# Seven products of a Winograd group in another order on TensorE, its copies and one weight split a step later

## The chip, the cores and the metric

The kernel runs on one core of a Trainium2 chip. The metric is the time of one execution in device microseconds (us). A core has four computing engines that work through queues of their own and wait for each other by semaphores: TensorE (PE in the profile: matmuls into PSUM; its weight loads are shown apart as PEld), VectorE (DVE), ScalarE (ACT) and GpSimd (POOL). SyncE (SP) issues DMAs. PE, DVE, ACT and SP execute their instructions in the order in which the kernel records them.

## The reference

One layer of an encoder over 320 rows (256 of a new stream, 64 of a running one, which share all weights), D_MODEL = 2048, D_FF = 5632:

```python
proj = rmsnorm(x, norm_mix) @ w_in                 # q k v, u v_s, g_a g_b
a  = stick_breaking(q, k, v)                       # 8 heads x 128
bb = spatial_gate(gelu(u), rmsnorm(gelu(vs)))
merged = sigmoid(g_a) * (a @ w_branch_a) + sigmoid(g_b) * (bb @ w_branch_b)
h  = x + merged @ w_out
gu = rmsnorm(h, norm_ffn) @ w_gate_up
h  = h + (silu(gu[..., :D_FF]) * gu[..., D_FF:]) @ w_down
return rmsnorm(h, norm_final), k, v, vs
```

All is float32. The change lies in the last product pair, `w_gate_up` and `w_down`.

## The kernel before

Features lie on partitions and the T = 320 rows on the free axis. A weight block is 128 output columns by K rows. Float32 weights arrive by DMA as a raw tile of 128 x 2048 (`raw`) and are split into two float16 halves that add up to the scaled weight: ScalarE makes the high half (`high`, L381) and VectorE the low half (`low`, L384), both into one tile `w`, of which there are three (`SPLIT`). A power-of-two scale comes first: ScalarE sums absolute values (`bound`, L211, written to `junk`), VectorE packs the result (`pack`, L217 and L219, tile `packed`), TensorE spreads it over partitions (`spread`, L223, tile `row`), VectorE turns it into `up` and `down` (`close`, L227 to L229). Activations are split into float16 halves in the same way. An ordinary block (`Group.block`) then takes three products per 128 rows of K, at L109 to L111.

Some pairs of blocks go through a class of their own, `Fast`: a Winograd form of a 2 x 2 block product. A group takes two blocks (gate and up of one column block, or two blocks of `w_down`) with 16 (or 12) pieces of K, and uses sums of weight pieces (`sum_up`, L425, VectorE, four sums, tile `sum`) and of activations (`mix`, tile `mix`). There are 40 groups: a run of 8 with gate and up; a run of 18, of which the first 6 are of `w_down` (a down group) and 12 of gate and up (an up group); a run of 4 down and 8 up groups; and two down groups with K = 12 x 128 that stand alone between ordinary blocks, near the end. Of a group TensorE makes nine pieces, which get short names here:

- chain products, all accumulated in one half of the PSUM tile `acc` ("first" in the code): A1 (weight as it is), A2 (with sum 2), A3 (with sum 3)
- the other product B (with sum 1), in the other half of the same PSUM tile
- G, the high halves of the gate block in whole (L429), G1 and G2, products into the first and second half of the gate's PSUM tile (an `aux`); U and U1, the same for the up block's tile (another `aux`)

A1, A2, A3, B, G1, G2 and U1 are 16 matmuls of 160 columns each (L435, `cross`); G and U are 16 matmuls of 320 columns (L429, `whole`). ScalarE reads the chain between its products: copy K0 after A1 and copy K1 after A2 (`keep_state`, L440, tile `seen`), copy K2 after A3, negated, into the up block's tile (L442), and copy KB of B's half (`take_other`, L478, tile `bb`). K2 comes before U, which accumulates on it. VectorE joins the copies to the products afterwards (`join`, L482 to L485); then up groups take Silu on ScalarE (L1212) and a product on VectorE (L1220), and down groups add both results to the residual on VectorE (L1228, twice).

The order of each queue is made by a step counter. `tick()` advances it and records the actions that were put at that step with `at(step, action, rank)`, in the order of their ranks; an action that is called outright stands where the code reaches it. A Fast group takes four steps, with a `tick()` at the end of each. `at(s - 3, self.high, ...)` thus puts a high half three steps before its group's start. A group's loads are recorded 11 and 10 steps ahead of its start, its two `bound` 9 and 7, its `pack`, `spread` and `close` 7, 5 and 4 steps ahead.

Of the kernel before, what the change touches and what calls it, by code (L numbers as in the profile page):

```python
# [13 lines left out]
AF = mybir.ActivationFunctionType  # L14
ALU = mybir.AluOpType

P = 128
TP = 256
TS = 64
T = TP + TS  # L20
# [32 lines left out]
def stream_step(ctx: ExitStack, tc: tile.TileContext, xT, w_in, w_a, w_b, w_out, w_gu, w_down,  # L53
                gains, ws_t, bs, ck_t, cv, y_t, k_t, v_t, sv_t):
    nc = tc.nc
# [8 lines left out]
    def acc():  # L64
        return psum.tile([P, 512], F32, tag="acc", bufs=3, name="acc")

    def aux():
        return psum.tile([P, 512], F32, tag="aux", bufs=4, name="aux")
# [8 lines left out]
    def at(tick, fn, *a, rank=5):  # L77
        if tick <= state["tick"]:
            fn(*a)
        else:  # L80
            later.setdefault(tick, []).append((rank, fn, a))

    def tick():
        state["tick"] += 1
        for _, fn, a in sorted(later.pop(state["tick"], ()), key=lambda x: x[0]):
            fn(*a)

    def after(n, fn, *a, rank=5):
        if n == 0:
            fn(*a)  # L90
        else:
            at(state["tick"] + n, fn, *a, rank=rank)
# [20 lines left out]
    class Plain:  # L113

        def __init__(self, src, nk, start):
            self.src, self.nk, self.start, self.w = src, nk, start, {}
            for j, k0 in enumerate(range(0, nk, HALF)):
                at(start + j - 8, self.load, j, rank=0)
                at(start + j - 2, self.high, j, rank=1)
                at(start + j - 1, self.low, j, rank=1)  # L120
# [25 lines left out]
    def slot(shape=(T,), dt=F32R, name="S"):  # L146
        return big.tile([P, *shape], dt, tag="S", bufs=SLOTS, name=name)
# [28 lines left out]
    def t320(tag, bufs=2, dt=F32):  # L176
        return tmp.tile([P, T], dt, tag=tag, bufs=bufs, name=tag)
# [219 lines left out]
    class Fast(Group):  # L397
# [3 lines left out]
        def __init__(self, units, n, start, undo, late_undo=False):  # L401
            self.units, self.undo_of, self.w, self.raw, self.sums, self.start = units, undo, {}, {}, {}, start
            self.n, self.half = n, n // 2
            self.width = [n * P] * 2
            for u, src in enumerate(units):
                s = start + u
                at(s - 11, self.load, u, src, 0, n, rank=0)
                at(s - 9 + u, self.bound, u, False, rank=0.9 if u else 4)
                at(s - 3, self.high, u, rank=2)
                at(s - 2, self.low, u, rank=2)  # L410
            at(start - 7, lambda: self.scale.pack(), rank=3)
            at(start - 5, lambda: self.scale.spread(), rank=1)
            at(start - 4, self.close, late_undo, rank=0.5)
            if late_undo:
                at(start, self.settle, rank=1)
            part = lambda u, j: self.w[u][2][:, :, j * self.half * P : (j + 1) * self.half * P]
            at(start, lambda: self.sum_up(1, part(1, 0), part(1, 1)), rank=2)
            at(start, lambda: self.sum_up(2, part(0, 0), self.sums[1]), rank=3)
            at(start + 1, lambda: self.sum_up(3, part(0, 0), part(1, 0)), rank=0.6)
            at(start + 1, lambda: self.sum_up(4, part(0, 1), self.sums[2]), rank=0.7)  # L420
# [3 lines left out]
            self.sums[i] = t[:, :, : self.half * P]  # L424
            nc.vector.tensor_tensor(out=self.sums[i], in0=a, in1=b, op=ALU.add)  # L425

        def whole(self, ps, u, x, r=None, start=True):
            for k in range(self.n) if r is None else r:
                nc.tensor.matmul(ps[:, :T], self.w[u][0][:, k * P : (k + 1) * P], x.half[k][0], start=start and k == 0,  # L429
                                 stop=False, skip_group_check=True)  # L430

        def cross(self, out, w, j, x, t, start=False, stop=True):
# [12 lines left out]
        def blocks(self, x):  # L445
            assert state["tick"] == self.start
            first, gate, self.up = acc(), aux(), aux()
            part = lambda ps, n: ps[:, n * N : (n + 1) * N]
            if self.n < KD:
                self.seen = slot((2, N), F32, "seen")  # L450
            else:
                turn_of["seen"] = turn_of.get("seen", 0) + 1
                self.seen = tmp.tile([P, 2, N], F32, tag="seen" if turn_of["seen"] % 2 else "sq", bufs=1, name="seen")
            self.chain, self.other = part(first, 0), part(first, 1)
            w0, w1, s, n = self.w[0][2], self.w[1][2], self.sums, self.half
            at(self.start + 2, self.take_other, rank=0.7)
            at(self.start + 2, self.keep_state, 2, rank=0.8)
            self.cross(self.chain, w0, 0, x, 11, start=True)
            self.keep_state(0)
            self.whole(gate, 0, x)  # L460
            self.cross(part(gate, 0), w0, n, x, 21)
            tick()
            self.cross(self.chain, s[2], 0, x, 2)
            self.keep_state(1)
            self.cross(self.other, s[1], 0, x, 1)
            self.cross(self.chain, s[3], 0, x, 3)
            tick()
            self.cross(part(gate, 1), s[4], 0, x, 22)
            self.whole(self.up, 1, x, range(n), False)
            tick()  # L470
            self.whole(self.up, 1, x, range(n, 2 * n), False)
            self.cross(part(self.up, 0), w1, n, x, 4)
            tick()
            return gate[:, :T], self.up[:, :T]
# [461 lines left out]
    start = base + 2 * WHOLE  # L936
    for i, (kind, n) in enumerate(line):
        by_vector = (0,) if 4 <= i < 33 and i % 5 in (1, 3) or i > 40 and i % 3 == 2 else ()
        if kind == "in":
            g = Group([[(w_in[n][:, j * HALF * P : (j + 1) * HALF * P], HALF) for j in range(2)]], start, lambda: [mixed.undo], 11, by_vector)  # L940
        else:
            g = Group([[(w_a[n], H), (w_b[n], H)]], start, lambda: [aT.undo, bT.undo], 11, by_vector, True)
# [3 lines left out]
    whole = Acts(KD)  # L946
# [5 lines left out]
    def block16(n, x):  # L952
        g = groups.pop(("in", n))
        return g.block(0, x), g.undo
# [15 lines left out]
    for i, (name, b, h) in enumerate(heads):  # L970
# [14 lines left out]
        else:  # L985
            ps, undo = block16(b * H + h, mixed.half)
# [16 lines left out]
    for g in range(H):  # L1003
        ps, undo = block16(4 * H + g, mixed.half)
# [67 lines left out]
    for g in range(H):  # L1072
        ps, undo = block16(3 * H + g, mixed.half)
        at(state["tick"] + 1, lambda g=g, ps=ps, undo=undo: nc.scalar.activation(
            out=us[g], in_=ps, func=AF.Gelu_apprx_tanh, scale=undo), rank=2)
# [24 lines left out]
    for m in range(KD):  # L1100
        g = groups.pop(("ab", m))
# [3 lines left out]
        for i, x in enumerate((aT, bT)):  # L1105
            ps = g.block(0, x.half, i * H, H)
# [18 lines left out]
    for made, (kind, s, i) in enumerate(order):  # L1125
        s0, n = SLICES[s]
# [11 lines left out]
        else:  # L1138
            if i % 2 == 0:
                undo = lambda s=s: [acts[s].undo]  # L1140
                if i in FAST_DOWN[s]:
                    g = Fast([w_down[j][:, s0 * P : (s0 + n) * P] for j in (i, i + 1)], n, now, undo, True)
                else:
                    g = Group([pieces(w_down[i], s0, n), pieces(w_down[i + 1], s0, n)], now, undo, 11, (), True, True)
# [21 lines left out]
    for m in range(KD):  # L1166
        x = t320("ev")
        nc.sync.dma_start(out=x, in_=xT[:, m, :])
        ps = outs[m].block(merged) if m < WHOLE_OUT else outs[m].block(0, whole.half)
# [34 lines left out]
    def gated(s, pg, pu, g):  # L1204
        fast = isinstance(g, Fast)
        t, u = g.join(pg, pu) if fast else (t320("ev"), t320("bb"))
        if g is None:
            nc.vector.tensor_tensor(out=t, in0=pg, in1=got["rh"], op=ALU.mult)
            nc.scalar.activation(out=t, in_=t, func=AF.Silu)
            nc.vector.tensor_tensor(out=u, in0=pu, in1=got["rh"], op=ALU.mult)  # L1210
        elif fast:
            after(1, lambda: nc.scalar.activation(out=t, in_=t, func=AF.Silu, scale=g.undo), rank=0.5)  # L1212
        else:
            nc.scalar.activation(out=t, in_=pg, func=AF.Silu, scale=g.undo)
            nc.scalar.activation(out=u, in_=pu, func=AF.Copy, scale=g.undo)

        def out():
            r = slot(dt=F32, name="act")
            if fast:
                nc.vector.scalar_tensor_tensor(out=r, in0=u, scalar=g.undo, in1=t, op0=ALU.mult, op1=ALU.mult)  # L1220
            else:
                nc.vector.tensor_tensor(out=r, in0=u, in1=t, op=ALU.mult)
            acts[s].add(r)

        after(1, out, rank=3)

    def downed(s, i, ps, g):
        nc.vector.scalar_tensor_tensor(out=hs[i], in0=ps, scalar=g.undo, in1=hs[i], op0=ALU.mult, op1=ALU.add)  # L1228
# [26 lines left out]
    for kind, s, i in order:  # L1255
        if kind == "up":
            if i < PLAIN:
                gate_w, up_w = groups.pop((kind, s, i))
                pg, pu, g = gate_w.block(hg), up_w.block(hg), None
            else:  # L1260
                g = groups.pop((kind, s, i))
                pg, pu = g.blocks(ffn) if isinstance(g, Fast) else (g.block(0, ffn.half), g.block(1, ffn.half, bank=aux))
            at(state["tick"] + 1, gated, s, pg, pu, g, rank=2)
            continue
        end = s == 2 and i == KD - 1
        g, u = groups.pop((kind, s, i))
        if isinstance(g, Fast):
            if u == 0:
                ps = g.blocks(acts[s])
                at(state["tick"] + 1, downed_pair, s, i, *ps, g, rank=2)  # L1270
            continue
        if not end:
            ps = g.block(u, acts[s].half)
# [20 lines left out]
        if end:  # L1294
            ps = g.block(u, acts[s].half, into=into)
# [123 lines left out]
```

## Time and profile before

| | us |
|---|---|
| three runs: lowest, median, highest | 1603.80, 1605.57, 1608.05 |
| the profiled execution | 1603.87 |
| its span (2.07 lies around it) | 1601.8 |
| PE busy in the span | 1563.3 (98%) |
| DVE busy | 1262.5 (79%) |
| ACT busy | 1145.7 (72%) |
| POOL busy | 118.2 (7%) |

The mean granted TensorE clock is 0.996. Busy time of PE counts from a matmul's start to its modelled end, and matmuls overlap: a 160-column matmul is shown with 233 ns and is followed 69 ns later by the next. A row of the timeline gives the start, the length, the engine, the line with its operation, the tiles (out<-in), the count of merged instructions, and in brackets the idle time before the first of them with what ended it.

### The profile page before, as it was taken

How to read it: one execution, taken by the hardware profiler on the slowest of the kernel's cores; microseconds unless marked ns; L12 is line 12 of the kernel's file. 1: busy time of each engine (PE TensorE's matmuls, PEld its weight loads, DVE VectorE, ACT ScalarE, POOL GpSimd, SP SyncE). 2: the span in 40 equal slices, each digit the busy share in tenths (PEclk: the TensorE clock that was granted, in tenths of full speed). 3: DMA queues.
4: the chain of work that ended last, by engine and by line, in shares of the span. 5: the costliest groups of instructions: out<-in, count | busy, mean ns of one | idle time of the engine just before them, and what ended most of it. 6: DMA issues, size and time to landing. Idle time of an engine off the chain costs nothing.

```text
span 1601.8 us, 32604 instructions
## 1 busy us (share of the span) xinstructions
PE 1563.3 (98%) x13603; PEld 1262.4 (79%) x13603; DVE 1262.5 (79%) x2149; ACT 1145.7 (72%) x1435; POOL 118.2 (7%) x144
## 2 busy tenths in 40 slices
PE   9999999999999999999999999999999999999997
PEld 9987777777777768879778877888888778887775
DVE  6789887977777766966869858899997688987785
ACT  6589888867666644846767778677776876777773
POOL 0110111100000000221000000000100000000000
PEclk9999999999999999999999999999999999999998
DMA  8567765644444444654544444445444544445341
GB/s 305 202 196 220 197 174 147 193 162 158 159 160 162 162 144 149 204 170 158 203 156 165 159 161 167 147 159 182 165 175 144 173 163 159 159 158 165 122 136 67
DMA packets 89012, 268.63 MB, mean 168 GB/s; under 512 B 27712, under 2 KB 34112, under 8 KB 79136
## 3 DMA queue, kind: packets, MB, share of 16 engines
q1 hardware_dynamic: 86416, 261.36, 49.2%
q0 software_dynamic: 1312, 3.80, 0.7%
q8 instruction: 106, 1.74, 0.4%
q10 hardware_dynamic: 1136, 1.39, 0.2%
q14 instruction: 42, 0.34, 0.1%
HBM read 256.03 MB, written 5.51 MB: 163 GB/s over the span
## 4 chain that ended last, share of the span: by engine, by line
PE 86%; ACT 7%; DVE 4%; issue 2%; DMA 1%; DVEq 0%; POOL 0%; ACTq 0%
PE acc L109 16%; PE acc L111 16%; PE acc L110 16%; PE acc L435 11%; PE aux L429 10%; PE aux L435 7%; ACT w L381 2%; PE aux L109 2%; PE aux L110 2%; PE aux L111 2%; PE aux L573 2%; DVE w L384 1%; ACT junk L211 1%; PE acc L573 1%; ACT seen L440 1%
## 5 line engine op out<-in xcount | busy, mean ns | idle before, releaser
L384 DVE SCALAR_TENSOR_TENSOR w<-raw,up,w 128x2048 f16<-128x2048 f32 (+1 forms) x216 | 498.6, 2308 | 116.7 <-ACT w L381 115.9
L111 PE MATMUL acc<-half,w 128*128 128x320 f16 x1920 | 574.1, 299 | 1.2 <-DVE w L384 1.1
L109 PE MATMUL acc<-half,w 128*128 128x320 f16 x1920 | 574.2, 299 | 0.4 <-DVE gate L1088 0.3
L110 PE MATMUL acc<-half,w 128*128 128x320 f16 x1920 | 574.1, 299 | 0.0
L381 ACT ACTIVATE w<-raw,up 128x2048 f16<-128x2048 f32 (+1 forms) x216 | 424.1, 1964 | 185.8 <-PE acc L111 144.8
L211 ACT ACTIVATE junk<-raw 128x2048 uint8<-128x2048 f32 (+1 forms) x190 | 354.8, 1867 | 5.3 <-DMA raw<-w_out 2.4
L111 PEld LDWEIGHTS <-w 128*128 128x128 f16 x2128 | 208.2, 98 | 82.6 <-DVE w L384 1.8
L109 PEld LDWEIGHTS <-w 128*128 128x128 f16 x2128 | 208.2, 98 | 82.0 <-issue 1.5
L110 PEld LDWEIGHTS <-w 128*128 128x128 f16 x2128 | 208.2, 98 | 77.2 <-issue 0.9
L435 PEld LDWEIGHTS <-sum 128*128 128x128 f16 x2528 | 178.7, 98 | 27.7 <-issue 27.7
L429 PE MATMUL aux<-half,w 128*128 128x320 f16 x1264 | 186.6, 299 | 0.0
L435 PE MATMUL acc<-mix,sum 128*128 128x160 f16 x1896 | 145.5, 234 | 22.3 <-ACT seen L440 22.3
L429 PEld LDWEIGHTS <-w 128*128 128x128 f16 x1264 | 120.0, 98 | 40.7
L435 PEld LDWEIGHTS <-w 128*128 128x128 f16 x1896 | 136.0, 98 | 6.4
L227 DVE TENSOR_REDUCE peak<-row 128x1 f32<-128x128 f32 x156 | 44.5, 285 | 93.1 <-PE row L223 92.9
L425 DVE TENSOR_TENSOR sum<-w,sum 128x2048 f16<-128x2048 f16 (+1 forms) x80 | 96.6, 1207 | 1.6
L425 DVE TENSOR_TENSOR sum<-w 128x2048 f16<-128x2048 f16 (+1 forms) x80 | 96.3, 1204 | 0.3
L372 POOL TENSOR_TENSOR undo<-down,undo 128x1 f32<-128x1 f32 x40 | 37.4, 936 | 527.3 <-DVE down L228 515.7
L131 ACT CAST w<-raw 128x1024 fp32r<-128x1024 f32 x36 | 37.6, 1046 | 44.8 <-PE acc L111 29.5
L109 PE MATMUL aux<-half,w 128*128 128x320 f16 x208 | 62.2, 299 | 0.0
L110 PE MATMUL aux<-half,w 128*128 128x320 f16 x208 | 62.2, 299 | 0.0
L111 PE MATMUL aux<-half,w 128*128 128x320 f16 x208 | 62.2, 299 | 0.0
(268 smaller groups left out, 1954.6 us busy)
## 6 DMA issues: line engine op xcount, KB each, us to landing
raw<-w_in SPq DMA_DIRECT2D x141, 512.0 KB, 4.7
raw<-w_gu SPq DMA_DIRECT2D x56, 1024.0 KB, 4.8
raw<-w_gu SPq DMA_DIRECT2D x64, 512.0 KB, 4.6
raw<-w_down SPq DMA_DIRECT2D x20, 1024.0 KB, 4.9
raw<-w_down SPq DMA_DIRECT2D x36, 512.0 KB, 3.9
raw<-w_out SPq DMA_DIRECT2D x32, 512.0 KB, 4.9
raw<-w_a SPq DMA_DIRECT2D x16, 512.0 KB, 3.8
raw<-w_b SPq DMA_DIRECT2D x16, 512.0 KB, 4.6
```

Source lines behind the costliest of these rows:

```text
L109: nc.tensor.matmul(ps[:, :T], a, x[0], start=first, stop=False, skip_group_check=True)
L110: nc.tensor.matmul(ps[:, :T], a, x[1], start=False, stop=False, skip_group_check=True)
L111: nc.tensor.matmul(ps[:, :T], b, x[0], start=False, stop=last, skip_group_check=True)
L131: nc.scalar.copy(out=self.w[j][0], in_=self.raw[:, j * HALF * P : (j + 1) * HALF * P])
L211: nc.scalar.activation(out=junk, in_=src, func=AF.Abs, accum_out=self.tops[:, i : i + 1])
L227: nc.vector.tensor_reduce(out=top, in_=self.row[:, :P], axis=mybir.AxisListType.X, op=ALU.max)
L381: nc.scalar.activation(out=w[:, 0], in_=self.raw[u][:, : self.width[u]], func=AF.Copy, scale=self.scale.up)
L384: nc.vector.scalar_tensor_tensor(out=self.w[u][1], in0=self.raw.pop(u)[:, : self.width[u]], scalar=self.scale.up, in1=self.w[u][0], op0=AL ...
L425: nc.vector.tensor_tensor(out=self.sums[i], in0=a, in1=b, op=ALU.add)
L429: nc.tensor.matmul(ps[:, :T], self.w[u][0][:, k * P : (k + 1) * P], x.half[k][0], start=start and k == 0, stop=False, skip_group_check=True)
L435: nc.tensor.matmul(out, w[:, h, (j + k) * P : (j + k + 1) * P], x.mixed[t, k][1 - h], start=start and k + h == 0, stop=stop and k + h == s ...
L573: nc.tensor.matmul(first[b][h][:, :T], w[:, (h * n + j) * P : (h * n + j + 1) * P], xs[c + j][i], start=not last and c + j + i == 0, stop= ...
```

## The change

In `blocks` the pieces stand in another order. Before: A1 G G1, step, A2 B A3, step, G2 and half of U, step, the other half of U and U1, step. After: A1 G, step, B A2, step, G1 A3, step, G2 U U1, step. `keep_state(1)` was called between A2 and B; it is now put at step 2 of the group. `keep_state(2)` and `take_other` go from step 2 to step 3, and change places. The high and the low half of the group's second block are made a step later, the low half with rank 1. Silu gets rank 0.9 in place of 0.5, and the product behind it comes two steps after the join in place of one.

```diff
@@ Fast.__init__
-                at(s - 3, self.high, u, rank=2)
-                at(s - 2, self.low, u, rank=2)
+                at(s - 3 + u, self.high, u, rank=2)
+                at(s - 2 + u, self.low, u, rank=1 if u else 2)
@@ Fast.blocks
-            at(self.start + 2, self.take_other, rank=0.7)
-            at(self.start + 2, self.keep_state, 2, rank=0.8)
+            at(self.start + 2, self.keep_state, 1, rank=0.8)
+            at(self.start + 3, self.keep_state, 2, rank=0.7)
+            at(self.start + 3, self.take_other, rank=0.8)
             self.cross(self.chain, w0, 0, x, 11, start=True)
             self.keep_state(0)
             self.whole(gate, 0, x)
+            tick()
+            self.cross(self.other, s[1], 0, x, 1)
+            self.cross(self.chain, s[2], 0, x, 2)
+            tick()
             self.cross(part(gate, 0), w0, n, x, 21)
-            tick()
-            self.cross(self.chain, s[2], 0, x, 2)
-            self.keep_state(1)
-            self.cross(self.other, s[1], 0, x, 1)
             self.cross(self.chain, s[3], 0, x, 3)
             tick()
             self.cross(part(gate, 1), s[4], 0, x, 22)
-            self.whole(self.up, 1, x, range(n), False)
-            tick()
-            self.whole(self.up, 1, x, range(n, 2 * n), False)
+            self.whole(self.up, 1, x)
             self.cross(part(self.up, 0), w1, n, x, 4)
             tick()
@@ gated
-            after(1, lambda: nc.scalar.activation(out=t, in_=t, func=AF.Silu, scale=g.undo), rank=0.5)
+            after(1, lambda: nc.scalar.activation(out=t, in_=t, func=AF.Silu, scale=g.undo), rank=0.9)
...
-        after(1, out, rank=3)
+        after(1 + fast, out, rank=3)
```

`whole` loses its range and its `start` argument: it now starts a PSUM tile for the first block alone (`start=u == k == 0`).

Behind `blocks` every line number of the changed kernel is one lower (L478 becomes L477, and so on). POOL's and SP's queues stand as before. Three places show what moves; the numbers behind the tile names tell buffers apart.

PE, around the end of A2 (sum_10053) in the second group of the first run; before:

```order
L435 LDWEIGHTS sum_10053
L435 MATMUL acc_10055<-mix_9578,sum_10053 128x160
L435 LDWEIGHTS sum_10053
L435 MATMUL acc_10055<-mix_9578,sum_10053 128x160
L435 LDWEIGHTS sum_10051
L435 MATMUL acc_10055<-mix_9305,sum_10051 128x160
```

and now:

```order
L435 LDWEIGHTS sum_10053
L435 MATMUL acc_10055<-mix_9578,sum_10053 128x160
L435 LDWEIGHTS sum_10053
L435 MATMUL acc_10055<-mix_9578,sum_10053 128x160
L435 LDWEIGHTS w_9904
L435 MATMUL aux_10056<-half_9050,w_9904 128x160
```

Behind A2 stood B (sum_10051), which writes the same PSUM tile acc_10055; now G1 stands there, which writes the gate's tile aux_10056.

PE, the spread of a later group's scale; before, in the middle of U:

```order
L429 LDWEIGHTS w_9985
L429 MATMUL aux_10057<-half_9048,w_9985 128x320
L223 LDWEIGHTS packed_10123
L223 MATMUL row_10210<-turner_91,packed_10123 128x128
L429 LDWEIGHTS w_9985
```

and now, between A3 (sum_10094) and G2 (sum_10096):

```order
L435 LDWEIGHTS sum_10094
L435 MATMUL acc_10055<-mix_9579,sum_10094 128x160
L223 LDWEIGHTS packed_10107
L223 MATMUL row_10181<-turner_91,packed_10107 128x128
L435 LDWEIGHTS sum_10096
L435 MATMUL aux_10056<-half_9050,sum_10096 128x160
```

The spread moved forward past G2 and half of U.

DVE, from one group's `pack` to the sums of the next; before:

```order
L219 TENSOR_SCALAR packed<-topmost 128x1
L384 SCALAR_TENSOR_TENSOR w<-raw,up,w 128x2048
L1220 SCALAR_TENSOR_TENSOR act<-aux,undo,ev 128x320
L384 SCALAR_TENSOR_TENSOR w<-raw,up,w 128x2048
L227 TENSOR_REDUCE peak<-row 128x1
L228 TENSOR_TENSOR down<-peak,bits 128x1
L229 TENSOR_TENSOR up<-down,bits 128x1
L425 TENSOR_TENSOR sum<-w 128x2048
L425 TENSOR_TENSOR sum<-w,sum 128x2048
```

and now:

```order
L219 TENSOR_SCALAR packed<-topmost 128x1
L384 SCALAR_TENSOR_TENSOR w<-raw,up,w 128x2048
L1219 SCALAR_TENSOR_TENSOR act<-aux,undo,ev 128x320
L227 TENSOR_REDUCE peak<-row 128x1
L228 TENSOR_TENSOR down<-peak,bits 128x1
L229 TENSOR_TENSOR up<-down,bits 128x1
L384 SCALAR_TENSOR_TENSOR w<-raw,up,w 128x2048
L425 TENSOR_TENSOR sum<-w 128x2048
L425 TENSOR_TENSOR sum<-w,sum 128x2048
```

The second low half and `close` changed places, so that the low half stands right before the first sum. Inside a run ScalarE's queue keeps its order but for K2, which now stands before KB.

More of the change, by code (lines that the diff above doesn't have):

```diff
@@ L425, in sum_up, with whole @@
             nc.vector.tensor_tensor(out=self.sums[i], in0=a, in1=b, op=ALU.add)
-        def whole(self, ps, u, x, r=None, start=True):
-            for k in range(self.n) if r is None else r:
-                nc.tensor.matmul(ps[:, :T], self.w[u][0][:, k * P : (k + 1) * P], x.half[k][0], start=start and k == 0,
+        def whole(self, ps, u, x):
+            for k in range(self.n):
+                nc.tensor.matmul(ps[:, :T], self.w[u][0][:, k * P : (k + 1) * P], x.half[k][0], start=u == k == 0,
                                  stop=False, skip_group_check=True)
```

## The prediction

> **What bounds the kernel now.** First the page, for the engine that is never idle; then the answer on ScalarE's copies (L440), for who waits for them; then the timeline of one period.
>
> ```profile
> PE 1563.3 (98%) x13603; PEld 1262.4 (79%) x13603; DVE 1262.5 (79%) x2149; ACT 1145.7 (72%) x1435; POOL 118.2 (7%) x144
> ```
>
> ```profile
> who waited for it (us, times):
>   PE acc L435: 22.3, 40
> ```
>
> TensorE is the bound: 38.5 us of the span are not busy. 22.3 of them are one wait, once in each of the 40 groups, for a copy of the chain. Next a down group in the second run, all engines; the brackets give the idle time ahead.
>
> ```profile
> 1055.45 2.35 DVE L384 SCALAR_TENSOR_TENSOR w<-raw,up,w 128x2048 f16<-128x2048 f32 x1 [0.65 <-ACT w L381]
> 1057.13 1.27 PE L435 MATMUL acc<-half,w 128*128 128x160 f16 x16
> 1057.72 0.28 DVE L227 TENSOR_REDUCE peak<-row 128x1 f32<-128x128 f32 x1
> 1058.24 2.34 PE L429 MATMUL aux<-half,w 128*128 128x320 f16 x16
> 1058.31 1.22 DVE L425 TENSOR_TENSOR sum<-w 128x2048 f16<-128x2048 f16 x1
> 1058.44 0.29 ACT L440 COPY seen<-acc 128x160 f32<-128x160 f32 x1 [1.13 <-PE acc L435]
> 1059.56 1.22 DVE L425 TENSOR_TENSOR sum<-w,sum 128x2048 f16<-128x2048 f16 x1
> 1060.41 1.27 PE L435 MATMUL aux<-half,w 128*128 128x160 f16 x16
> 1060.71 1.22 DVE L425 TENSOR_TENSOR sum<-w 128x2048 f16<-128x2048 f16 x1
> 1061.52 1.27 PE L435 MATMUL acc<-mix,sum 128*128 128x160 f16 x16
> 1061.84 1.22 DVE L425 TENSOR_TENSOR sum<-w,sum 128x2048 f16<-128x2048 f16 x1
> 1062.83 0.29 ACT L440 COPY seen<-acc 128x160 f32<-128x160 f32 x1 [0.30 <-PE acc L435]
> 1062.98 0.48 DVE L482 TENSOR_TENSOR ev<-aux,seen 128x320 f32<-128x320 f32 x1
> 1063.17 2.37 PE L435 MATMUL acc<-mix,sum 128*128 128x160 f16 x32 [0.38 <-ACT seen L440]
> 1065.07 0.16 DVE L219 TENSOR_SCALAR packed<-topmost 128x1 bf16<-128x1 f32 x1
> 1065.38 1.27 PE L435 MATMUL aux<-half,sum 128*128 128x160 f16 x16
> 1065.58 0.29 ACT L478 COPY bb<-acc 128x160 f32<-128x160 f32 x1 [2.46 <-PE acc L435]
> 1066.12 1.99 ACT L381 ACTIVATE w<-raw,up 128x2048 f16<-128x2048 f32 x1
> 1067.44 0.10 PEld L223 LDWEIGHTS <-packed 128*128 128x128 bf16 x1
> 1068.14 2.35 DVE L384 SCALAR_TENSOR_TENSOR w<-raw,up,w 128x2048 f16<-128x2048 f32 x1 [0.64 <-ACT w L381]
> 1069.82 1.27 PE L435 MATMUL acc<-half,w 128*128 128x160 f16 x16
> ```
>
> A1 starts at 1057.13 and the next group's A1 at 1069.82: a period of 12.69. A2 starts at 1061.52, K1 reads its end at 1062.83, and B with A3 (x32) starts at 1063.17: B hides nothing, it waits as A3 would, since it writes the PSUM tile that K1 reads. A product of 160 columns takes 1.11 from start to start (1060.41 to 1061.52), A2 takes 1.65. So the wait costs 0.54, not the 0.38 shown: the pipeline empties as well, 0.16. A period without it is 12.15. VectorE, though, is idle for only 0.64 of it: it is the second bound, and close.
>
> **The change part by part**, against the profiled execution (1603.87, span 1601.8); the median of three runs, 1605.57, is 1.7 higher, and the forecast goes to that.
>
> The chain products. With G at 2.17 (1058.24 to 1060.41) the new order counts from A1 at 0: G 1.11, B 3.28, A2 4.39, G1 5.50, A3 6.61, spread 7.72, G2 7.78, U 8.89, U1 11.06, end 12.15. B waits for K0, ready at 1.60 (1058.44 + 0.29 less 1057.13). K1 starts 0.20 behind A2's end as before (1062.83 is 5.70 into its group) and is done at 5.99; A3 comes at 6.61, so G1 covers it with 0.62 to spare. K2 starts 0.04 after A3's last result (1065.58 against 1063.17 + 2.37), so at 7.92; it and KB take 0.54 together (1065.58 to 1066.12), so it is done before 8.46, and U comes at 8.89: G2 covers it with 0.4 to spare or more. Gain 0.54 a group, where ScalarE is in time. It is: in an up group, where its queue is fullest, these rows stand (the group starts at 836.88):
>
> ```profile
> 840.28 1.99 ACT L381 ACTIVATE w<-raw,up 128x2048 f16<-128x2048 f32 x1
> 842.57 0.29 ACT L440 COPY seen<-acc 128x160 f32<-128x160 f32 x1 [0.30 <-PE acc L435]
> 843.66 0.56 ACT L1212 ACTIVATE ev<-ev,undo 128x320 f32<-128x320 f32 x1 [0.79 <-DVE ev L484]
> 844.02 0.16 DVE L219 TENSOR_SCALAR packed<-topmost 128x1 bf16<-128x1 f32 x1
> ```
>
> The high half ends at 5.39, 0.3 ahead of K1. Silu, behind K1 and ahead of K2, waits for VectorE's join until 6.78 and ends at 7.34, still before K2 can start at 7.92.
>
> 34 of the 40 groups show 0.38, the first and the last of them here: 34 x 0.54 = 18.4.
>
> ```profile
> 842.92 2.37 PE L435 MATMUL acc<-mix,sum 128*128 128x160 f16 x32 [0.38 <-ACT seen L440]
> 1450.02 2.37 PE L435 MATMUL acc<-mix,sum 128*128 128x160 f16 x32 [0.38 <-ACT seen L440]
> ```
>
> The second block's halves, a step later. ScalarE's queue in a run stays the same, so the high half starts 0.58 after A3's result as before (1066.12), at 8.46, and the low half at 10.48 (1068.14, 2.60 after it). Its tile is that of this group's first block, which G1 now reads until 6.61: 1.8 ahead, no wait. Before, the first sum starts 2.86 after the low half (1055.45 to 1058.31), 0.59 of which is `close` (from 1057.72). VectorE will do `close` ahead of the low half, in its idle 0.64, so that the sum comes 2.27 to 2.45 after it. B needs sum 1 at 3.28, where it is done at about 2.0 (10.48 - 12.15 + 2.45 + 1.22). Raw tiles come free with the low halves, at the same place of a group, and SP's and POOL's queues stand as before: no load is later.
>
> The spread, moved forward 2.7 on TensorE (10.31 into the group at 1067.44, now its weights are wanted at 7.72 - 0.13 = 7.59). It waits for `packed`, and A3's result, through the high half, low half, sums and join, sets `packed` of the next group: 10.48 + 2.45 + 4.67 (1058.31 to 1062.98) + 2.25 (to 1065.07 + 0.16) = 19.85 after the group's start, which must not exceed the period + 7.59. That gives a period of 12.26, with 0.05 for the semaphore 12.31, in the 10 groups that join a down group's results: a loss of 0.16 each, 1.6. An up group has `packed` 0.8 sooner (844.02 is 7.14 into its group, 1065.07 is 7.94): no loss. The ends are 0 (the low half takes 2.27, period 12.15) and 0.4 (TensorE's own idle time comes back): 0 to 4 us. The 2.45 is from a run's last group, where a sum with a wait for VectorE itself stands right behind the low half, as it now does in all groups:
>
> ```profile
> 911.34 2.35 DVE L384 SCALAR_TENSOR_TENSOR w<-raw,up,w 128x2048 f16<-128x2048 f32 x1 [1.12 <-ACT w L381]
> 913.79 1.23 DVE L425 TENSOR_TENSOR sum<-w 128x2048 f16<-128x2048 f16 x1
> ```
>
> The two sums that wait for the one before (1058.31 to 1059.56, 1.25) against one that doesn't (1060.71 to 1061.84, 1.13) say the same. [...]
>
> The three ends of runs. There K1 is late for another reason:
>
> ```profile
> 913.02 1.27 PE L435 MATMUL acc<-half,w 128*128 128x160 f16 x16
> 916.97 2.00 ACT L381 ACTIVATE w<-raw,up 128x2048 f16<-128x2048 f32 x1 [2.35 <-DVE up L229]
> 920.77 0.27 ACT L440 COPY seen<-acc 128x160 f32<-128x160 f32 x1
> 921.09 2.37 PE L435 MATMUL acc<-mix,sum 128*128 128x160 f16 x32 [2.42 <-ACT seen L440]
> ```
>
> ScalarE waits for the next, ordinary pair's `up`, which VectorE makes after two sums; the order of these stays. TensorE goes on at 8.07 into the group. Before, that stood against B's due 5.50, now against A3's 6.61: 1.47 of the 2.58 stay, 1.11 go, 3.3 in three.
>
> The first group of all, and one of the two lone ones:
>
> ```profile
> 823.77 1.27 PE L435 MATMUL acc<-half,w 128*128 128x160 f16 x16
> 830.23 2.37 PE L435 MATMUL acc<-mix,sum 128*128 128x160 f16 x32 [0.80 <-ACT seen L440]
> 831.46 0.48 DVE L1222 TENSOR_TENSOR act<-bb,ev 128x320 f32<-128x320 f32 x1
> 1545.19 1.82 PE L435 MATMUL acc<-mix,sum 128*128 128x160 f16 x24 [0.66 <-ACT seen L440]
> ```
>
> The first lost 0.80 + 0.16. K1 released TensorE at 830.23, and A3 is due at 823.77 + 6.61 = 830.38: in time. But an ordinary up pair runs ahead of it, and the sum that ScalarE takes of that pair's product (L1222) now stands before K2 in its queue. The product ends at 831.94, the sum takes some 0.6 (Silu on as many columns 0.56), K2 some 0.45 (less than the 0.54), so U starts at 833.0 and was due at 823.77 + 8.89 = 832.66: 0.37 comes back, 0.6 is gained. The lone ones lost 0.66 + 0.16 each: with 12 pieces of K, B was due at 4.13 (0.75 x 5.50) and ran at 4.95, and A3 is due at 4.96. So 1.6 is gained.
>
> Sum: 18.4 - 1.6 + 3.3 + 0.6 + 1.6 = 22.3. The profiled time becomes 1581.6, the median 1583.
>
> **The rivals.**
>
> - VectorE is the next bound. Its idle 0.64 in 12.69 says so for down groups; against it stands 1.12 in up groups (the row at 911.34). The spread's loop is 12.31 in down groups and 11.5 in up groups; were it 0.7 longer, they would take 13.0 and 12.2: 10 x 0.7 + 24 x 0.06 less, so 1591.
> - ScalarE's copies are late. Silu stands between K1 and K2 and waits for VectorE's join. If the join came 2 us later than worked out (its L484 done at 8.5 instead of 6.3), U would wait about 0.54, in some 26 up groups: 14 less, 1597. The idle 0.79 before Silu speaks for such a wait, its ending 0.6 before K2's start against it.
> - No change: A3 waits as B did, since the cost lies in the copy's reading a chain that goes on, and not in what stands between. G then hides nothing in the rows of before; yet A2 follows K0 with G and G1 between, and waits for nothing. 1605.
> - Slower: the second block's high half sits one step later, next to a `bound` (1.8 long: what stands between the high half's end at 918.97 and K1 at 920.77). If it got behind that on ScalarE, the spread's loop would grow to 14.1 in down groups and 13.3 in up groups, and 10 x 1.4 + 24 x 0.6 would be lost: with the 5.5 of the other groups gained, 1629. It decides from 0.4 (down) or 1.2 (up) of such lateness. The recorded order has it in front.
>
> **How the numbers follow.** A measurement tells this kernel from no change at about 0.3%, 4.8 us. The forecast's own case gets 0.70, with 1577 (all of 28.7 gone, the wait's 22.3 and 40 x 0.16) to 1588 (the spread costs 4 and an end or two gains nothing). VectorE as the bound 0.14, late copies 0.07, no change 0.05, slower 0.04. The first three are faster: 0.91. From 1577 to 1592 holds the first two.
>
> **What would show it.** In the changed trace the wait of PE for `seen` falls from 40 times, 22.3, to three of about 1.3 and next to nothing else. Up groups have a period of 12.15, down groups 12.15 to 12.31, where PE's row L223 waits for `packed` by 0.1 to 0.2. In the first group U waits for L442 by 0.2 to 0.4. VectorE's idle time ahead of the low half falls to 0.1 in down groups. I am wrong if a period in the middle of a run is over 12.4, with PE waiting for a sum, for `packed` or for L442; or if stalls appear in the ordinary blocks between the runs.

## The result, and the profile after

The changed kernel takes 1577.43 us (median of 4 runs, 1577.21 to 1577.62), the kernel before 1605.45 (4 runs, 1603.80 to 1608.05): a ratio of 0.9824, 95% interval 0.9807 to 0.9841. The gain is 28.0, the forecast said 22.3. The time lies at the low edge of the range. The profiled execution took 1577.21, its span is 1575.4, against 1603.87 and 1601.8 before.

The page's row of engines, and the answer on ScalarE's copies (L440):

```profile
PE 1555.8 (99%) x13603; PEld 1259.9 (80%) x13603; DVE 1267.2 (80%) x2149; ACT 1147.0 (73%) x1435; POOL 97.1 (6%) x144
```

```profile
who waited for it (us, times):
  PE acc L435: 3.5, 3
```

The wait that stood 40 times with 22.3 is left three times. The timeline of a down group in the second run, to be set beside the one shown of before:

```profile
1037.12 1.27 PE L435 MATMUL acc<-half,w 128*128 128x160 f16 x16
1038.23 2.34 PE L429 MATMUL aux<-half,w 128*128 128x320 f16 x16
...
1040.40 2.38 PE L435 MATMUL acc<-mix,sum 128*128 128x160 f16 x32
...
1042.61 1.27 PE L435 MATMUL aux<-half,w 128*128 128x160 f16 x16
1042.82 0.29 ACT L440 COPY seen<-acc 128x160 f32<-128x160 f32 x1 [0.30 <-PE acc L435]
...
1043.72 1.27 PE L435 MATMUL acc<-mix,sum 128*128 128x160 f16 x16
...
1044.60 0.16 DVE L219 TENSOR_SCALAR packed<-topmost 128x1 bf16<-128x1 f32 x1
1044.67 2.35 DVE L384 SCALAR_TENSOR_TENSOR w<-raw,up,w 128x2048 f16<-128x2048 f32 x1
1044.80 0.10 PEld L223 LDWEIGHTS <-packed 128*128 128x128 bf16 x1
1044.83 0.22 PE L223 MATMUL row<-turner,packed 128*128 128x128 bf16 x1
1044.88 1.27 PE L435 MATMUL aux<-half,sum 128*128 128x160 f16 x16
1045.03 0.42 ACT L442 ACTIVATE aux<-acc 128x320 f32<-128x320 f32 x1 [1.92 <-PE acc L435]
...
1045.99 2.34 PE L429 MATMUL aux<-half,w 128*128 128x320 f16 x16
1046.94 0.28 DVE L227 TENSOR_REDUCE peak<-row 128x1 f32<-128x128 f32 x1
...
1047.59 2.35 DVE L384 SCALAR_TENSOR_TENSOR w<-raw,up,w 128x2048 f16<-128x2048 f32 x1
...
1049.27 1.27 PE L435 MATMUL acc<-half,w 128*128 128x160 f16 x16
1049.98 1.23 DVE L425 TENSOR_TENSOR sum<-w 128x2048 f16<-128x2048 f16 x1
```

A1 to A1 is 12.15 (1037.12 to 1049.27), and no row of PE has an idle time in brackets. B and A2 are merged into one row (x32, both write `acc`). K1 is done at 1043.11 and A3 starts at 1043.72: 0.61 to spare, 0.62 was worked out. K2 is done at 1045.45 (1045.03 + 0.42), U starts at 1045.99: 0.54 to spare. All ordinary groups but one have this period, up groups and down groups alike; in one (A1 at 1073.57) it is 12.47. VectorE's rows in the group ahead of it:

```profile
1068.89 0.16 DVE L219 TENSOR_SCALAR packed<-topmost 128x1 bf16<-128x1 f32 x1
1069.35 2.35 DVE L384 SCALAR_TENSOR_TENSOR w<-raw,up,w 128x2048 f16<-128x2048 f32 x1 [0.29 <-issue]
```

The low half starts 0.46 behind `packed`, where it is 0.07 in the group above, and the profile shows nothing that it waited for.

At the end of the second run, ScalarE and TensorE:

```profile
1211.35 2.00 ACT L381 ACTIVATE w<-raw,up 128x2048 f16<-128x2048 f32 x1 [2.22 <-DVE up L229]
...
1215.15 0.27 ACT L440 COPY seen<-acc 128x160 f32<-128x160 f32 x1
...
1215.47 1.27 PE L435 MATMUL acc<-mix,sum 128*128 128x160 f16 x16 [1.18 <-ACT seen L440]
```

The stall of 2.42 is now 1.18 (1.17 and 1.18 at the other two ends), with the emptied pipeline 1.34 where it was 2.58. In the first group of all, the row ahead of U and U itself:

```profile
831.00 1.27 PE L435 MATMUL aux<-half,sum 128*128 128x160 f16 x16
832.39 2.33 PE L429 MATMUL aux<-half,w 128*128 128x320 f16 x16
```

1.39 instead of the usual 1.11: U is 0.28 late there, behind K2 (ScalarE's L442 runs from 831.92 to 832.34).

### The profile page after: what moved, and what is told of

It reads as the page before. It is cut to its first block, busy times and chain, and to the rows that moved or that the text cites. A ratio compares the mean times of both kernels' runs of the same rounds, so it can differ in the third digit from the quotient of the medians.

```text
span 1575.4 us, 32634 instructions
## 1 busy us (share of the span) xinstructions
PE 1555.8 (99%) x13603; PEld 1259.9 (80%) x13603; DVE 1267.2 (80%) x2149; ACT 1147.0 (73%) x1435; POOL 97.1 (6%) x144
## 3 DMA queue, kind: packets, MB, share of 16 engines
q10 hardware_dynamic: 1136, 1.39, 0.3%
## 4 chain that ended last, share of the span: by engine, by line
PE 86%; ACT 6%; DVE 5%; issue 2%; DMA 0%; POOL 0%; DVEq 0%; ACTq 0%
PE acc L109 17%; PE acc L111 17%; PE acc L110 17%; PE acc L435 10%; PE aux L429 9%; PE aux L435 7%; ACT w L381 2%; DVE w L384 2%; PE aux L109 2%; PE aux L110 2%; PE aux L111 2%; PE aux L572 2%; ACT junk L211 1%; DVE sum L425 1%; PE acc L572 1%
## 5 line engine op out<-in xcount | busy, mean ns | idle before, releaser
L211 ACT ACTIVATE junk<-raw 128x2048 uint8<-128x2048 f32 (+1 forms) x190 | 355.3, 1870 | 5.3 <-issue 1.9
L440 ACT COPY seen<-acc 128x160 f32<-128x160 f32 x80 | 23.3, 292 | 52.2 <-PE acc L435 52.1
```

The lines of the kernel that those rows point to most:

```text
L211: nc.scalar.activation(out=junk, in_=src, func=AF.Abs, accum_out=self.tops[:, i : i + 1])
```

## The experiments

### 1. The kernel before, with a tile of its own for B

```diff
-            self.chain, self.other = part(first, 0), part(first, 1)
+            self.chain, self.other = part(first, 0), part(acc(), 0)
...
-            self.cross(self.other, s[1], 0, x, 1)
+            self.cross(self.other, s[1], 0, x, 1, start=True)
```

> The kernel before, with its own order of products, copies and halves; only B gets a PSUM tile of its own (of the three acc tiles), so that it no longer writes the tile that K1 reads. Theory (the 0.54 a group was a wait of B for K1, because they share a tile): B starts right behind A2 and covers K1, the period of an ordinary group falls from 12.69 to 12.15 with no piece moved, the wait of PE for seen falls from 40 times to the 3 run ends (about 1.3 each), and the time is 1577 to 1582, close to the changed kernel's 1577.4. Rival (the cost lies in reading a chain that goes on, whatever stands between): B or A3 still waits, period 12.4 to 12.69, time 1592 to 1605.

Measured: 1577.26 (4 runs, 1576.95 to 1578.76), ratio 0.9827 to the kernel before, 0.9813 to 0.9840: the whole gain, with no piece moved. PE's waits for K1 in the answer on waits (us in total, times, the longest), and a group's chain:

```profile
PE acc L435 <- ACT seen L440: 3.3, 3, 1.1
```

```profile
1055.31 3.48 PE L435 MATMUL acc<-mix,sum 128*128 128x160 f16 x48
1056.62 0.29 ACT L440 COPY seen<-acc 128x160 f32<-128x160 f32 x1 [0.30 <-PE acc L435]
```

A2, B and A3 run on as one row of 48 matmuls while K1 reads: B covers K1. So the 0.54 a group was a wait for the tile, not a price of reading a chain that goes on. The rival "no change" of the prediction falls with it. The one run that stands 1.4 to 1.8 above the other three is the profiled one; of that more below.

### 2. The order of products and copies alone

```diff
-                at(s - 3 + u, self.high, u, rank=2)
-                at(s - 2 + u, self.low, u, rank=1 if u else 2)
+                at(s - 3, self.high, u, rank=2)
+                at(s - 2, self.low, u, rank=2)
```

(against the changed kernel)

> The changed kernel with the second block's halves where the kernel before has them (steps -2 and -1 of the group); order of products, copies, Silu and act product as changed. Theory (the halves' move is needed, since the second high half now stands between K1 and K2 on ScalarE): in down groups it waits for G1 to free its tile until about 6.7, ends at 8.7 and K2 at 9.1, so U (due 8.89) starts about 0.3 late; in up groups Silu stands ahead of it until 7.34, it ends at 9.33, K2 at 9.76, and U is about 0.9 late. 10 x 0.3 + 24 x 0.9 = 25 of the gain are lost: time 1597 to 1605, PE waiting for L442 in nearly every ordinary group. Rival (the order of products alone makes the gain): 1577 to 1580.

Measured: 1584.10 (4 runs, 1584.02 to 1584.39), 6.7 above the changed kernel. A down group, ScalarE and then TensorE:

```profile
1057.34 0.29 ACT L440 COPY seen<-acc 128x160 f32<-128x160 f32 x1 [0.30 <-PE acc L435]
1058.45 2.00 ACT L381 ACTIVATE w<-raw,up 128x2048 f16<-128x2048 f32 x1 [0.81 <-PE aux L435]
1060.36 0.42 ACT L442 ACTIVATE aux<-acc 128x320 f32<-128x320 f32 x1
```

```profile
1051.65 1.27 PE L435 MATMUL acc<-half,w 128*128 128x160 f16 x16
...
1059.41 1.27 PE L435 MATMUL aux<-half,sum 128*128 128x160 f16 x16
1060.83 2.33 PE L429 MATMUL aux<-half,w 128*128 128x320 f16 x16
...
1064.10 0.30 PE L435 MATMUL acc<-half,w 128*128 128x160 f16 x2
```

The high half waits 0.81 for G1, K2 stands behind it, and U comes 0.31 late (1059.41 to 1060.83 is 1.42 in place of 1.11): period 12.45 (1051.65 to 1064.10). That is the mechanism expected, and in down groups the size. In up groups the period is the same, where 0.9 of lateness was expected: with the low half earlier the sums and the join come earlier too, Silu no longer waits long, and it is through before G1 has freed the tile. At the ends of runs this kernel has no wait for K1, since `up` comes earlier as well; 34 x 0.31 less 3 x 1.34 and 0.5 more in the first group come to 7.0 (10.5 - 4.0 + 0.5), near the 6.7 measured. So the halves' move is needed for a quarter of the gain.

### 3. The halves a step later, alone and with the act product

Alone, against the kernel before:

```diff
-                at(s - 3, self.high, u, rank=2)
-                at(s - 2, self.low, u, rank=2)
+                at(s - 3 + u, self.high, u, rank=2)
+                at(s - 2 + u, self.low, u, rank=1 if u else 2)
```

> The kernel before with the second block's high and low halves a step later and nothing else. Theory (the halves' move gains nothing by itself; ScalarE's queue in a run stays as it is, and the spread sits at 10.3 of the group, where VectorE's loop has 2.6 to spare): the period stays 12.69, PE waits 40 times for seen, time 1603 to 1607. Rival (the halves' move gains part of the 28 us): 1582 to 1600, period under 12.6.

Measured: 1630.98 (4 runs, 1630.14 to 1631.82), 26 slower than before, ratio 1.0159 (1.0145 to 1.0173). Neither theory had that: the expectation took ScalarE's queue to stay, and it didn't. ScalarE in an up group, and PE's wait for sums:

```profile
1137.72 0.43 ACT L442 ACTIVATE aux<-acc 128x320 f32<-128x320 f32 x1
1139.69 0.47 ACT L211 ACTIVATE junk<-act 128x320 uint8<-128x320 f32 x1 [1.54 <-DVE act L1220]
1140.07 0.19 ACT L211 ACTIVATION_READ_ACCUMULATOR junk<-act 128x1 f32 x1
1140.16 1.99 ACT L381 ACTIVATE w<-raw,up 128x2048 f16<-128x2048 f32 x1
```

```profile
PE acc L435 <- DVE sum L425: 15.9, 20, 1.1
```

The sum that ScalarE takes of the finished product (L211, `junk<-act`) got in front of the second high half, since it is still recorded a step earlier than that now is. It waits for VectorE, whose next work waits for the high half. Up groups grow to 13.65; down groups, which have no such sum, stay at 12.69. If this is all, the product has to come a step later too, as the change has it:

```diff
-        after(1, out, rank=3)
+        after(1 + fast, out, rank=3)
```

> The kernel before with two parts of the change: the second block's halves a step later, and the act product two steps behind the join in place of one. With the halves alone the up groups had a period of 13.65, with ScalarE idle 1.54 ahead of the sum over the act tile (L211 junk<-act), which then stood in front of the second high half. Theory (that sum was the whole of the loss; with the product a step later the high half is again in front of it): ScalarE's queue in a run is that of the kernel before, period 12.69 in up groups, time 1603 to 1607. Rival (the later halves cost by themselves, through the low half next to the sums): period over 12.8, time 1612 to 1631.

Measured: 1606.67 (10 runs, 1603.81 to 1609.46), ratio 1.0002 (0.9992 to 1.0012): nothing. The wait for sums is gone, what is left is that of before:

```profile
PE acc L435 <- ACT seen L440: 22.6, 40, 2.4
```

### 4. Run ends

Against the changed kernel, for the ordinary pair that follows a run (`late`) and for the product of the pair ahead of the first group (`g.ahead`):

```diff
-                at(s - 3, self.high, u, rank=2)
-                at(s - 2, self.low, u, rank=2)
+                at(s - 3 + late, self.high, u, rank=0.85 if late else 2)
+                at(s - 2 + late, self.low, u, rank=1 if late else 2)
...
-        after(1 + fast, out, rank=3)
+        after(1 + (fast or g is not None and g.ahead), out, rank=3)
```

> The changed kernel, and besides: in the last group of each of the three runs the following ordinary pair's first high half comes behind K1 on ScalarE (a step later, ahead of Silu) and its low half a step later; and the product that an ordinary pair leaves for the first group of all comes a step later, behind K2. Theory (K1 is late at the run ends only because of the high half in front of it, which waits for up): K1 starts at 5.7 of the group as elsewhere, A3 waits for nothing; the high half ends at about 8.0, Silu at 8.5, K2 at 8.95, so U starts 0.1 to 0.2 late: 1.1 to 1.2 gained three times, and 0.28 in the first group, 3.5 to 3.9 together; time 1573.5 to 1574. Rival (VectorE is next: the first low half and the split behind it come 2 us later and the following ordinary blocks wait): the gain comes back there, 1576 to 1580.

Measured: 1573.38 (5 runs, 1572.97 to 1573.60), ratio 0.9800 to the kernel before (0.9787 to 0.9813), 4.05 below the changed kernel. The gain is a little more than the 3.5 to 3.9 expected, and nothing comes back as the rival had it. The same run end as above:

```profile
1212.09 0.29 ACT L440 COPY seen<-acc 128x160 f32<-128x160 f32 x1 [2.19 <-PE acc L435]
1212.28 2.00 ACT L381 ACTIVATE w<-raw,up 128x2048 f16<-128x2048 f32 x1
1214.18 0.55 ACT L1211 ACTIVATE ev<-ev,undo 128x320 f32<-128x320 f32 x1
1214.64 0.42 ACT L442 ACTIVATE aux<-acc 128x320 f32<-128x320 f32 x1
```

K1 now waits for TensorE (2.19), not TensorE for K1; PE has no idle time in any of the 40 groups, but for 0.13 in one. U isn't late at this run end either: the run's last group has no spread, and K2 comes in time.

### 5. How much room VectorE has

Two more instructions of VectorE in each group, behind the fourth sum:

```diff
+    extra = const.tile([P, 1], F32, name="extra")
+    more_work = lambda: nc.vector.tensor_reduce(out=extra, in_=ident, axis=mybir.AxisListType.X, op=ALU.max)
...
-            at(start + 1, lambda: self.sum_up(4, part(0, 1), self.sums[2]), rank=0.7)
+            at(start + 1, lambda: (self.sum_up(4, part(0, 1), self.sums[2]), more_work(), more_work()), rank=0.7)
```

> The changed kernel with two more VectorE instructions in each Fast group, behind the fourth sum (a maximum over a 128 x 128 tile each, written to a tile that nobody reads; some 0.2 to 0.3 each from start to start, E together). Theory (in a down group VectorE's loop from A3's result to the next spread has 0.03 to spare, in an up group some 0.8, and VectorE is idle there for 0.43): the period of the 10 ordinary down groups grows by E - 0.03, with PE waiting for packed at L223, up groups stay at 12.15: with E = 0.5 4.7 in all, time 1581 to 1583. Rival 1 (the down groups have slack like the up groups): 1577 to 1578. Rival 2 (up groups are as tight): 34 x 0.47 = 16, time 1593.

Measured: 1582.34 (4 runs, 1582.20 to 1582.67), 4.9 above the changed kernel. VectorE's two instructions, and PE's wait for `packed` (lines are two higher here):

```profile
1056.64 0.60 DVE L200 TENSOR_REDUCE extra<-ident 128x1 f32<-128x128 f32 x2
1057.16 0.48 DVE L483 TENSOR_TENSOR ev<-aux,seen 128x320 f32<-128x320 f32 x1
```

```profile
PE row L225 <- DVE packed L221: 3.0, 10, 0.3
```

E is 0.52. The 10 groups that stand right behind a down group, and join its results, take 12.60 to 12.65, 0.47 more, and wait 0.3 each at the spread (0.46 with the emptied pipeline); the others stay at 12.15, but for one of 12.37 at the start of the first run. So VectorE's loop has 0.05 to spare behind a down group and at least 0.52 behind an up group.

### 6. The stall at the run ends and the clock

The traces of before and after differ by one thing that no wait explains. Between the last group's A1 in the second run and the next Fast group the changed kernel saves 1.63 more than behind the first run (95.00 to 92.12 against 93.36 to 92.11), and there the granted clock in the trace of before falls to 0.50 (1230.92 to 1234.33). So the stall was brought back into the changed kernel, by before's order in the last group of each run alone, and in the kernel before it was taken out (the part of experiment 4's edit that bears on the run ends, with rank 0.6). The first of these two, where the pieces of the last group are put in order:

```diff
...
+            self.last and self.cross(part(gate, 0), w0, n, x, 21)
             tick()
-            self.cross(self.other, s[1], 0, x, 1)
+            self.last or self.cross(self.other, s[1], 0, x, 1)
             self.cross(self.chain, s[2], 0, x, 2)
+            self.last and (self.keep_state(1), self.cross(self.other, s[1], 0, x, 1), self.cross(self.chain, s[3], 0, x, 3))
...
```

> The changed kernel with the order of before's products in the last group of each of the three runs alone (K1 called between A2 and B, as before), which brings back the stall of TensorE of 2.42 there. Theory (each such stall may be followed by 3.41 us at a granted clock of 0.5, 1.7 lost, as the trace of before shows once at 1230.9; whether it is depends on where a window falls): the base is 1577.4 + 3 x 1.25 = 1581.2, and single runs stand 0, 1.7, 3.4 or 5.1 above it, with a granted clock that falls by 0.001 for each: a scatter of over 1.5, median 1581 to 1584. Rival (the scatter of before, 1603.5 to 1608, has nothing to do with these stalls): all runs within 0.6 of each other, 1580.9 to 1581.6, clock 0.997 to 0.998.

> The kernel before with the ordinary pair's first high half behind K1 and Silu at the run ends (and its low half a step later), so that the three stalls of 2.42 go and 40 small waits stay; U then waits for K2 behind that high half by some 0.5. Theory (the scatter comes from these stalls): 3 x (2.58 - 0.54 - 0.6) = 4.3 less work time, no drop of the clock before the tail, runs within 0.6 of each other, at 1602.2 - 4.3 = 1597.9, clock 0.997 to 0.998. Rival (the clock drops for other reasons): runs scatter by 3 or 4 as before, median 1600 to 1602.

Measured, each run with its mean granted clock:

| kernel | runs |
|---|---|
| changed | 1577.21, 1577.41 (0.998), 1577.44, 1577.62 (0.997) |
| changed, stall back | 1582.68 (0.997), 1583.75 (0.996), 1585.90, 1586.10 (0.995) |
| before, 21 runs beside the experiments | 1601.68, 1603.46 (0.997), 1603.80 (0.996), nine of 1604.99 to 1605.96 (0.995, once 0.996), nine of 1606.51 to 1607.18 (0.994) |
| before, stalls out | 1597.84, 1597.88, 1598.12 (0.997), 1597.96 (0.998) |

The scatter comes and goes with the stalls, 5.5 and 3.4 with those of 2.1 to 2.4 us, 0.4 and 0.3 without, and the clock with it (0.994 to 0.997 against 0.997 and 0.998). The median with the stall back is 1584.82, above the 1581 to 1584 expected; its profiled run has three drops, and 3 x 1.7 above 1581.2 is 1586.3. Without stalls the kernel before is at 1597.92 (expected 1597.9), with 40 small waits, and holds within 0.3.

What follows is read from stretches of 3.41 us, the length of the drop in before. In that trace drops begin at 1230.92 and, when TensorE is done, at 1592.73, 106 x 3.4133 apart; in that of the changed kernel with the stall back they begin at 918.21, 1218.58 and 1447.28, 88 and 67 x 3.4133 apart. So the stretches are counted in each trace from where its drops begin. Before, and the changed kernel with the stall back (columns: us, busy time of PE and the other engines, PEclk, share and rate of the DMA):

```profile
916.89:920.31 3.42, 1.78 (x26) 1.65 (x24) 3.38 (x7) 3.34 (x2) 1.23 (x1) 1.00 0.41 147
920.31:923.72 3.41, 2.63 (x39) 2.63 (x39) 2.82 (x4) 1.41 (x6) 0.00 (x0) 1.00 0.07 12
1227.51:1230.92 3.41, 0.99 (x15) 0.86 (x13) 3.38 (x5) 3.07 (x5) 0.00 (x0) 1.00 0.00 0
1230.92:1234.33 3.41, 3.41 (x29) 3.41 (x27) 1.29 (x4) 0.37 (x2) 0.00 (x0) 0.50 0.43 119
...
1463.03:1466.44 3.41, 1.69 (x25) 1.69 (x25) 3.34 (x7) 2.13 (x4) 0.00 (x0) 1.00 0.01 2
1466.44:1469.86 3.42, 3.42 (x40) 2.93 (x38) 0.39 (x1) 2.70 (x5) 0.00 (x0) 1.00 0.74 226
```

```profile
1215.17:1218.58 3.41, 1.28 (x19) 1.15 (x17) 3.38 (x6) 3.41 (x4) 0.59 (x1) 1.00 0.23 93
1218.58:1221.99 3.41, 3.25 (x25) 3.25 (x25) 2.20 (x4) 0.57 (x2) 0.00 (x0) 0.50 0.21 59
```

The stall of 2.42 in the first and third run of before is cut by a stretch's edge (920.31 and 1463.03), and 1.64 and 1.72 of it fall into one stretch: no drop. In the second run the stretch holds all of it (busy 0.99), and the stretch behind runs at 0.50: 1.7 lost.

## Why the prediction came out as it did

- **The cause** was right: B waited for K1 with the tile (experiment 1), 34 x 0.54 = 18.4 stands in the trace to 0.1.
- **The spread's loop** was mis-sized: a loss of 1.6 was forecast, 0.3 came, in the one group of 12.47. TensorE waits for `packed` there (L223 at 1081.59, 0.15 idle), because the low half of the group ahead started late. By the prediction's own sign (a period over 12.4, with a wait for `packed`) this group counts against it. The late start isn't chance: the traces of experiment 4 and of the changed kernel with the stall back have it at the same place (0.29 and 0.28 idle, periods 12.46 and 12.44). Its cause stays open. The loop itself is there, with 0.05 to spare instead of 0.16 too little (experiment 5). Two terms of the sum were too large. From the low half to the sum it takes 2.39 (1047.59 to 1049.98), not 2.45. And the weights of the spread aren't wanted 0.13 ahead of it: in the group shown above the load starts 0.03 before its matmul (1044.80, 1044.83), 0.04 after `packed` (1044.60 + 0.16), and in the group of 12.47, where TensorE does wait for `packed`, 0.01 before it (1081.58, 1081.59), 0.05 after `packed` (1081.37 + 0.16).
- **A wait of VectorE for itself** shows 0.12 in these rows: behind the group's other low half `close`, which waits for nothing of VectorE, starts 2.27 later (1044.67 to 1046.94), while the sum that waits for its low half starts 2.39 later, 0.12 more. These two followers differ in kind, but the sums alone say the same: in the next group one that waits for the sum ahead starts 1.26 behind it (1049.98 to 1051.24), one that doesn't 1.14 (1051.24 to 1052.38). That there was hardly a loss is owed to the two terms above.
- **The run ends** gave 1.24 each (2.58 to 1.34), 3.7 instead of 3.3; 1.47 was to stay. The high half started there 0.13 sooner against the group than before, as its wait for `up` shows: 2.22 in place of 2.35.
- **The first group** gave 0.68 (period 13.11 before, 12.43 now), 0.6 forecast, with 0.28 coming back at U as the prediction placed it (it says 0.37; its own figures, 833.0 less 832.66, give 0.34). **The lone groups** gave 0.86 each, from A1 to U1 (9.16 to 8.30 and 9.10 to 8.24): 1.7, forecast 1.6.
- **The clock** was missed. Those terms add up to 24.2 (18.4 - 0.3 + 3.7 + 0.7 + 1.7), the profiled spans differ by 26.4. 1.6 of the rest is the drop behind the second run's end, and 0.5 is gone already before the first Fast group (A1 at 823.77 before, 823.24 now), where nothing was moved: the halves alone (experiment 3) and before with the stalls out, both with before's order there, have their first K0 at 824.7 and 824.8, before at 825.1 and the changed kernel at 824.5, so this is scatter. From median to median it is 28.0: the profiled run of before has one drop and a clock of 0.996, and most of the 21 runs have 0.995 or 0.994, which speaks for two or three (a drop takes half of 3.41 out of 1600, 0.001). So the step of the prediction that missed most is the one that took the three ends at the length of their stall alone. That the time still lies in the range is in part luck: its low edge, 1577, stood for the whole wait gone, and 4.0 of that stayed at the run ends; without the clock, the terms as measured lead to 1605.45 - 24.2 = 1581.3.
- **VectorE as the next bound** (0.14) was near: its idle 0.64 in down groups is gone, and 0.52 more of work costs 4.9 (experiment 5). **Late copies** (0.07) didn't come: no ordinary group waits for L442. **Slower** (0.04) named the right danger, the second high half behind something else in ScalarE's queue, and the price (1629): experiment 3 has it, at 1631, with another instruction in front, in the kernel before and mostly in up groups, so the nearness of the two times is chance. The change avoids it by the act product's extra step, which the prediction passed over.

## What to carry to other kernels

Look first at what two instructions share before moving one away from the other: here a second PSUM tile, two edited lines, gave what the new order of seven products with all that it drags along gave (1577.26 against 1577.43). Where steps of a queue are moved, take each part of the move by itself: one part alone cost 26, since a small reduction slipped in front of a long instruction that everybody waits for. And a long stall can cost more than its length: the one of 2.42 in the second run of before took 1.63 more.

## What the runs showed of the hardware

Four stalls of TensorE were followed in these traces by a slow stretch, which cost a further 1.7 each (half of 3.41). Cut into stretches as above, the traces of before and after and the three run ends of the changed kernel with the stall back have, up to the tail, four stretches that began at full clock and in which TensorE was idle for more than 2 us: 2.42 in before, 2.25, 2.13 and 2.28 with the stall back. Each was followed by 3.41 us at a granted clock of 0.50. The most idle one that wasn't is that of 1.72 in before; the most in the changed kernel is 1.18. Between 1.72 and 2.13 lies no case.

The profiled run of experiment 1 has a stall of 2.0 in an early stage (`aux` L751 waits for `S`; 1.6 in before). Its first K0 comes at 826.5, where before, the changed kernel, experiments 2 and 4, the halves alone and before with the stalls out have it at 824.5 to 825.1, and its mean clock is 0.997. That a drop of the clock lies ahead of this K0 is an estimate from these numbers.

Idle time isn't the whole condition. In the tail of the changed kernel the clock falls behind a stretch with 3.01 idle (1565.82 to 1569.23), in that of before behind one with 0.35, which has matmuls of one column (L1311) in it:

```profile
1589.32:1592.73 3.41, 3.06 (x24) 2.66 (x21) 1.21 (x6) 1.73 (x6) 0.31 (x1) 1.00 0.00 0
```

What else decides isn't shown. Single executions of before lie between 1601.68 and 1608.05, those with the stall back between 1582.68 and 1586.10; kernels without stalls of 2 us or more hold within 0.3 to 0.6 (0.3 before with the stalls out, 0.4 in the changed kernel, 0.6 in experiment 4). That the wide scatter comes from where the stretches lie against the stalls is the author's estimate: only one execution of each kernel has a trace.
